# Making the key product's input mixtures between the tiles of rates, in the second half of a two-layer trunk

## The chip, the cores and the metric

The kernel runs on one core of a Trainium2 chip (trn2). The metric is the device time of one execution in microseconds. The kernel before the change takes 2615.0 us, the median of 3 runs (2613.59 to 2615.41). The profiled execution is a run of its own: it took 2623.95 us, and its span from the first to the last instruction is 2621.8 us, at a mean granted TensorE clock of 0.965.

## The reference: what is computed

The input is 1024 frames of 1024 channels. Layer 0 is an RWKV-7 time mixer, layer 1 a diagonal state-space layer. Each is followed by a dense MLP with a squared ReLU, and each of the four sub-layers ends in a layer norm. The change lies in the projections of the time mixer:

```python
xx = jnp.pad(x, ((0, 0), (1, 0), (0, 0)))[:, :-1] - x      # the frame before, less this one
xr = x + xx * mu[0]
xw = x + xx * mu[1]
xk = x + xx * mu[2]
xv = x + xx * mu[3]
xa = x + xx * mu[4]
xg = x + xx * mu[5]
r = xr @ wr
w_pre = (w0 + jnp.tanh(xw @ w1) @ w2).astype(f32)
k = xk @ wk
v = xv @ wv
a = jax.nn.sigmoid(a0 + (xa @ a1) @ a2)
g = jax.nn.sigmoid(xg @ g1) @ g2
```

The decay `w` and the rate `a` come from two small products in a row ("rates" below), the gate `g` likewise ("gates"), and `r`, `k`, `v` each from one 1024 x 1024 product of a mixture of each frame with the frame before it. A recurrence over the frames (`lax.scan`) then uses r, w, k, v and a, head by head.

## The kernel before, in words

**Layout.** Channels lie on the 128 partitions, so that 1024 channels are 8 tiles, and frames lie along the free axis. The frames are worked off in two halves (H = 0 and 1) of 512. A float32 product is made as three fp32r matmuls: each operand is split into a high and a low part (`split`, L152: ScalarE casts the high part in L153, VectorE or GpSimd subtracts it in L154), and `mm3` (L201) multiplies high by high, high by low and low by high. Nearly all matmuls are recorded at L199.

**Projections.** `rwkv_proj(H)` (L253) makes one half's r, w, k, v, a and g and stores them in DRAM. In the second half it works in this order:

1. It splits the 8 tiles of x into operands (L313), and makes three first small products of x (`scaled` L319, `shifted` L334, `gate_c` L360, `gate_a` L379), whose results are the operands `hx` (for the rates), `gx` and `h2` (for the gates).
2. `rates(n)` (L393) for n = 0 to 7: six matmuls of half depth into two PSUM tiles, a Tanh (L404) and a scaling (L349) on ScalarE for each of the two, and two stores (L389).
3. `gate(n)` (L408) for n = 0 to 7: four matmuls, a copy on ScalarE (L421), a store.
4. The key product: `mixes(2)` (L287) makes the 8 mixtures, one per tile of channels, and `squares` (L432) multiplies them with two column blocks of the weight at a time (48 matmuls for a pair, evacuated by L442). Then the same for r with `mixes(0)`, and last for v with `mixes(3)`.

**One mixture** (`mixes`, L287 to L301): ScalarE multiplies the tile by 1 - mu (L290). For odd tiles VectorE adds mu times the shifted tile (L292, one instruction). For even tiles ScalarE makes mu times the shifted tile in a second buffer (L295) and GpSimd adds the two (L296). Then `operand(m)` splits the sum, so that ScalarE casts it to `oAh` (L153) and VectorE subtracts for `oAl` (L154). A mixture issues no DMA.

**Buffers.** `oAh` and `oAl` have 8 slots each. The operands of x fill all of them until the first small products are done. Then `hx`, `gx` and `h2` take three of `oAh`, which leaves five, and `hx` comes free after the last rate, `gx` and `h2` after the last gate. `m` has 2 slots. The tag `ev`, from which the second buffer of an even mixture and every evacuated rate or gate comes, has 4.

**Order.** The order in which the instructions stand in each engine's queue is not the written one. A planner of the framework (the kernel is built with `schedule_with_timeline_sim=True`) lays it out ahead of time: it takes ready instructions by priority, hands out slots, and goes by durations of its own. Priorities rise in the order of writing, and `rank(base)` (L89) starts a stretch at a given number, where a lower number goes first. `core()` (L801) ranks the recurrence of each eighth m (`elem` L514, `amat` L591, `invert` L627, `chain` L689, `gnorm` L745) at m x 10000 and a few thousand, and both halves' projections at 100000, the second half's being written at m = 3. So the projections are what fills the engines beside the recurrence. `wo(0)` (L968, rank 99000) and the first layer norm (L861, rank -1) follow for the first half, written at m = 5, and then the MLP.

Of the kernel before, what the change touches and what calls it, by code (L numbers as in the profile page):

```python
# [73 lines left out]
def trunk(ctx, tc, A):  # L74
# [13 lines left out]
    @contextmanager  # L88
    def rank(base):  # L89

        keep = tc.cur_priority
        tc.cur_priority = base
        yield
        tc.cur_priority = keep
# [19 lines left out]
    def vec(n, k):  # L114
        i = PV.index(n)
        return pv[:, i, k : k + 1]
# [35 lines left out]
    def split(src, hi, lo, e=None):  # L152
        S.copy(hi, src)  # L153
        (e or V).tensor_sub(lo, src, hi.bitcast(F32))  # L154
# [12 lines left out]
    def wload(src, kt, n, key=None):  # L167

        step = 512 // n
        out = []  # L170
        for k0 in range(0, kt, step):
            kept = low.get((key, k0)) if key else None
            raw = wp.tile([128, step, n], F32, tag="wraw", name="wraw", bufs=2)
            SP.dma_start(raw, src[:, k0 : k0 + step])
            hi = wp.tile([128, step, n], F32R, tag="whi", name="whi")
            lo = wp.tile([128, step, n], F32R, tag="wlo", name="wlo")
            nw[0] += 1
            if kept is not None:
                SP.dma_start(lo.bitcast(F32).rearrange("p k n -> p (k n)"), kept)
                S.copy(hi, raw)  # L180
            else:
                split(raw, hi, lo, G if nw[0] % WLG[0] in WLG[1] and WLG[2] <= nw[0] < WLG[3] else V)
                if key:
                    low[key, k0] = dr.tile([128, 512], F32, name=f"low{len(low)}")
                    SP.dma_start(low[key, k0], lo.bitcast(F32).rearrange("p k n -> p (k n)"))
            out += [(hi[:, k], lo[:, k]) for k in range(step)]
        return out
# [10 lines left out]
    def mmb(p, w, x, **kw):  # L198
        bulk.append((PE.matmul(p, w, x, **kw).ins, x.shape[-1]))  # L199

    def mm3(p, whi, wlo, xh, xl, first, last):  # L201
        mmb(p, whi, xh, start=first, stop=False)
        mmb(p, whi, xl, start=False, stop=False)
        mmb(p, wlo, xh, start=False, stop=last)
# [28 lines left out]
    def operand(src, H=0, e=None):  # L233
        h, l = optile(H, "h"), optile(H, "l")
        split(src, h, l, e)
        return h, l

    def psd():
        return pd.tile([128, HT], F32, tag="d", name="d")
# [13 lines left out]
    def rwkv_proj(H):  # L253
# [25 lines left out]
        def spare0():  # L279
            t = spare("vsa", 2, 2) + spare("vsa", 2, 2)  # L280
            for _ in range(4):
                t += spare("kbt", 1, KTB)
            t += [stash[:, k, l] for k in (1, 2, 3) for l in range(2)]
            t += spare("o", 1, OB) + spare("o", 1, OB)
            return [(t[2 * k], t[2 * k + 1]) for k in range(KT)]

        def mixes(j, dst=None):  # L287
            for k in range(KT):
                m = tp.tile([128, HT], F32, tag="m", name="m")
                S.mul(m, xs[k][:, 1:], mum[:, j, k : k + 1])  # L290
                if k % 4 in VM[H]:
                    V.scalar_tensor_tensor(m, xs[k][:, 0:HT], vec(f"mu{j}", k), m, op0=ALU.mult, op1=ALU.add)  # L292
                else:
                    m2 = tp.tile([128, HT], F32, tag="ev", name="m2", bufs=EVB)
                    S.mul(m2, xs[k][:, 0:HT], vec(f"mu{j}", k))  # L295
                    G.tensor_add(m, m, m2)  # L296
                if dst:
                    split(m, *dst[k])
                    yield dst[k]
                else:  # L300
                    yield operand(m)  # L301
# [13 lines left out]
        if H == 0:  # L315
            with rank(MIXR):
                xm = list(mixes(2))
# [30 lines left out]
        def half_sigmoid(t):  # L348
            S.activation(t, t, AF.Identity, bias=half, scale=0.5)  # L349
# [38 lines left out]
        def store_out(out, n, e):  # L388
            (ST if out in STO else SP).dma_start(scr[out][n * 128 : (n + 1) * 128, t0 : t0 + HT], e)  # L389
# [3 lines left out]
        def rates(n):  # L393

            if n % 4 == 0:
                w2[0] = wload(A["wa2"][:, n // 4], 4, 128, f"wa2{n}")
            pp = [psd(), psd()]
            for wi, xi in ((0, 0), (0, 1), (1, 0)):
                for j in range(2):
                    js = slice(64 * j, 64 * j + 64)  # L400
                    mmb(pp[j], w2[0][n % 4][wi][js], hx[xi][js], start=wi == 0 and xi == 0, stop=wi == 1)
            for j, out in ((0, "sg"), (1, "a")):
                e = tp.tile([128, HT], F32, tag="ev", name="ev", bufs=EVB)
                S.activation(e, pp[j], AF.Tanh, bias=pvh[:, j, n : n + 1], scale=0.5)  # L404
                half_sigmoid(e)
                store_out(out, n, e)

        def gate(n):  # L408
            if n % 4 == 0:
                wg[0] = wload(A["g2a"][:, n // 4], 4, 128, f"g2a{n}")  # L410
                rawb = wp.tile([128, 512], F32, tag="wraw", name="w2raw", bufs=2)
                SP.dma_start(rawb, A["g2b"][:, n * 128 : n * 128 + 512])
                wg[1] = wp.tile([128, 512], F32R, tag="whi", name="w2st")
                S.copy(wg[1], rawb)
                V.tensor_sub(wg[1][64:128], rawb[64:128], wg[1][64:128].bitcast(F32))
            q = n % 4
            p = psd()
            mm3(p, wg[0][q][0], wg[0][q][1], gx[0], gx[1], True, False)
            mmb(p, wg[1][:, q * 128 : (q + 1) * 128], h2, start=False, stop=True)
            e = tp.tile([128, HT], F32, tag="ev", name="ev", bufs=EVB)  # L420
            S.copy(e, p)  # L421
            store_out("g", n, e)

        def square(wn, out, xm, n):
            p = psd()
            w = [x for k0 in (0, 4) for x in wload(A[wn][n][:, k0 : k0 + 4], 4, 128, f"{wn}{n}-{k0}")]
            dense(p, w, xm)
            e = tp.tile([128, HT], F32, tag="ev", name="ev", bufs=EVB)
            S.copy(e, p)  # L429
            store_out(out, n, e)  # L430

        def squares(wn, out, xm, n):  # L432

            pp = [psd(), psd()]
            for k0 in (0, 4):
                ws = [wload(A[wn][n + j][:, k0 : k0 + 4], 4, 128, f"{wn}{n + j}-{k0}") for j in range(2)]
                for k in range(4):
                    for j in range(2):
                        mm3(pp[j], *ws[j][k], *xm[k0 + k], k0 + k == 0, k0 + k == KT - 1)
            for j in range(2):  # L440
                e = tp.tile([128, HT], F32, tag="ev", name="ev", bufs=EVB)
                S.copy(e, pp[j])  # L442
                store_out(out, n + j, e)

        if H == 0:

            km = xm
            with rank(MIX0R):
                rm = list(mixes(0, spare0()))
            for n in range(4):  # L450
                rates(n)
                square("wk", "k", km, n)
            for n in range(4):
                square("wr", "r", rm, n)
            yield
            for n in range(4, KT):
                rates(n)
                square("wk", "k", km, n)
            for n in range(4, KT):
                square("wr", "r", rm, n)  # L460
            if not GV:
                for n in range(KT):
                    gate(n)
        else:
            for n in range(KT):
                rates(n)
            for n in range(KT):
                gate(n)
            for j, wn, out in ((2, "wk", "k"), (0, "wr", "r")):
                xm = list(mixes(j))  # L470
                for n in range(0, KT, 2):
                    if n in (0, 2, 4, 6):
                        squares(wn, out, xm, n)
                    else:
                        square(wn, out, xm, n)
                        square(wn, out, xm, n + 1)
# [324 lines left out]
    def core():  # L801

        pg = rwkv_proj(0)
        next(pg)
        bulk.clear()
# [8 lines left out]
        for m in range(8):  # L814
            if m == PB:
                with rank(100000):
                    run(rwkv_proj(1))
# [700 lines left out]
    for c in range(2):  # L1518
        for b in range(JB - TB, JB):
            db(b, False, slice(256 * c, 256 * c + 256))  # L1520
        if c == 0:
            with rank(LN8R):
                early = last_norm(hB, 3, 0)
# [74 lines left out]
```

## Time and profile before

| | before |
|---|---|
| median of 3 runs | 2615.0 us |
| profiled execution: its time, its span | 2623.95 us, 2621.8 us |
| granted TensorE clock, mean | 0.965 |
| TensorE matmul, busy | 2483.8 us, 95% |
| VectorE, busy | 1812.8 us, 69% |
| ScalarE, busy | 1215.2 us, 46% |
| GpSimd, busy | 492.9 us, 19% |

PE is the matmul engine, DVE VectorE, ACT ScalarE, POOL GpSimd, SP SyncE, whose queue (SPq) issues the loads and stores. A row of the waits names the instruction that waited, the one that released it, the microseconds, how often and the longest. A row of stretches gives for each engine the busy microseconds and the instructions, then PEclk (the granted TensorE clock as a share of full speed), the share of time in which the DMA engines were busy, and GB/s. A row of groups gives line, engine, operation, tiles written and read, shapes and count, then busy us and mean ns of one, then the idle time ahead of them and what ended it. A row of the timeline starts with the start and the length in us. Times within the run count from the first instruction.

In that count, second-half rates are evacuated by ScalarE from 320.0 to 362.8 us, the second half's gates are evacuated until 376.6, the first pair of key columns is evacuated at 412.9 and 413.9, the last pair of r is stored at 541.2, and the last of v at 653.4.

### The profile page before, as it was taken

Reading aid. Unit: us, or ns where it says so; the run is one execution under the profiler, and the core shown is the slowest. Engines: PE = TensorE matmul, PEld = TensorE weight load, DVE = VectorE, ACT = ScalarE, POOL = GpSimd, SP = SyncE. Lnnn points to the kernel's source line nnn. Section 1 sums busy time; section 2 is a strip of 40 time slices with the busy share of each in tenths; the row PEclk is TensorE's granted clock in tenths of the full one; section 3 lists DMA queues with packets and bytes.
Section 4 is the critical chain, followed back from the end, with each engine's and each line's share of the span. In section 5 each row is a group of like instructions: output and inputs, shape, how many; then the busy total and the mean of one; then the engine's idle time right before and its main releaser. Section 6 shows DMA issues by size and latency. Waiting matters only on the chain.

```text
span 2621.8 us, 43716 instructions
## 1 busy us (share of the span) xinstructions
PE 2483.8 (95%) x16624; PEld 2013.9 (77%) x16624; DVE 1812.8 (69%) x3299; ACT 1215.2 (46%) x2171; POOL 492.9 (19%) x404
## 2 busy tenths in 40 slices
PE   7899979999989999999999999999999999999997
PEld 5778757788767787777787888887777888888876
DVE  7367767576987777899886555677687555555576
ACT  7554575555454443445543333433464333423344
POOL 3121442433431202001000000101212111111011
PEclk9998979988979999999999999999999999999998
DMA  4764555555322333446655333253222111111123
GB/s 145 257 215 153 169 186 171 181 172 172 105 64 84 97 91 105 162 121 157 182 195 181 96 96 97 93 178 136 93 85 83 54 49 53 53 49 57 49 93 116
DMA packets 207569, 320.72 MB, mean 122 GB/s; under 512 B 20352, under 2 KB 81920, under 8 KB 207360
## 3 DMA queue, kind: packets, MB, share of 16 engines
q1 hardware_dynamic: 206208, 315.84, 38.2%
q8 instruction: 131, 2.15, 0.3%
q10 hardware_dynamic: 1152, 2.10, 0.2%
q14 instruction: 78, 0.64, 0.1%
HBM read 253.89 MB, written 63.96 MB: 121 GB/s over the span
## 4 chain that ended last, share of the span: by engine, by line
PE 57%; DVE 9%; DMA 3%; issue 2%; ACT 2%; POOL 0%; SPq 0%; DVEq 0%; ACTq 0%; POOLq 0%
PE d L199 43%; PE d L1046 9%; DVE wlo L154 2%; DMA wraw<-in_mw_dram 1%; DMA s_y<-yg 1%; DVE hA L1009 1%; ACT hA L905 0%; PE pu L1318 0%; PE pbu L1330 0%; ACT whi L153 0%; PE py L1382 0%; PE py L1390 0%; DMA yl<-s_y 0%; DVE hB L904 0%; PE pk L1279 0%
## 5 line engine op out<-in xcount | busy, mean ns | idle before, releaser
L153 ACT CAST whi<-wraw 128x512 fp32r<-128x512 f32 x524 | 324.5, 620 | 678.0 <-PE d L199 429.3
L154 DVE TENSOR_TENSOR wlo<-wraw,whi 128x512 fp32r<-128x512 f32 x524 | 392.8, 750 | 251.9 <-ACT whi L153 244.6
L199 PE MATMUL d<-qbuf,whi 128*128 128x512 f32 (+1 forms) x1344 | 407.2, 386 | 13.1 <-DVE hA L1009 7.1
L199 PE MATMUL d<-oAh,whi 128*128 128x512 f32 (+1 forms) x768 | 310.9, 412 | 14.2 <-ACT ev L429 7.8
L199 PE MATMUL d<-oAh,wlo 128*128 128x512 f32 (+1 forms) x768 | 309.4, 408 | 7.2 <-DVE wlo L154 4.3
L199 PE MATMUL d<-oAl,whi 128*128 128x512 f32 (+1 forms) x768 | 309.0, 407 | 7.0 <-DVE oAl L154 7.0
L199 PEld LDWEIGHTS d<-qbuf,whi 128*128 128x128 f32 x1344 | 244.0, 188 | 69.1 <-DVE hA L1009 11.2
L199 PE MATMUL d<-qbuf,wlo 128*128 128x512 f32 (+1 forms) x672 | 255.7, 383 | 1.6 <-DVE wlo L154 1.4
L199 PE MATMUL d<-oBh,wlo 128*128 128x512 f32 x512 | 203.4, 398 | 3.5 <-DVE wlo L154 3.4
L199 PE MATMUL d<-oBh,whi 128*128 128x512 f32 x512 | 201.5, 394 | 2.3 <-ACT whi L153 2.2
L199 PE MATMUL d<-oBl,whi 128*128 128x512 f32 x512 | 200.2, 391 | 0.0
L199 PEld LDWEIGHTS d<-oAh,whi 128*128 128x128 f32 (+1 forms) x768 | 148.1, 195 | 50.2 <-ACT ev L429 10.0
L199 PEld LDWEIGHTS d<-oAh,wlo 128*128 128x128 f32 (+1 forms) x768 | 148.0, 194 | 41.2 <-DVE wlo L154 5.8
L199 PEld LDWEIGHTS d<-oAl,whi 128*128 128x128 f32 (+1 forms) x768 | 148.1, 194 | 39.8 <-DVE oAl L154 9.9
L199 PE MATMUL d<-qh,wlo 128*128 128x512 f32 x384 | 151.3, 394 | 0.0
L199 PE MATMUL d<-ql,whi 128*128 128x512 f32 x384 | 150.6, 392 | 0.0
L199 PE MATMUL d<-qh,whi 128*128 128x512 f32 x384 | 149.2, 389 | 0.0
L199 PEld LDWEIGHTS d<-qbuf,wlo 128*128 128x128 f32 x672 | 126.3, 188 | 28.3 <-DVE wlo L154 3.0
L1009 DVE TENSOR_TENSOR hB<-hB,d 128x512 f32<-128x512 f32 (+1 forms) x168 | 104.8, 632 | 30.1 <-PE d L199 28.2
L199 PEld LDWEIGHTS d<-oBh,wlo 128*128 128x128 f32 x512 | 96.2, 188 | 28.4 <-DVE wlo L154 6.1
L1009 DVE TENSOR_TENSOR hA<-hA,d 128x512 f32<-128x512 f32 x144 | 97.3, 680 | 28.1 <-PE d L199 27.0
L199 PEld LDWEIGHTS d<-oBh,whi 128*128 128x128 f32 x512 | 96.2, 188 | 23.7 <-ACT whi L153 2.8
(478 smaller groups left out, 5137.4 us busy)
## 6 DMA issues: line engine op xcount, KB each, us to landing
wraw<-in_mw_dram SPq DMA_DIRECT2D x376, 256.0 KB, 2.7
wraw<-in_glu_dram SPq DMA_DIRECT2D x64, 256.0 KB, 2.7
low<-wlo SPq DMA_DIRECT2D x52, 256.0 KB, 2.8
wlo<-low SPq DMA_DIRECT2D x52, 256.0 KB, 3.7
raw<-in_mw_dram SPq DMA_DIRECT2D x48, 256.0 KB, 2.6
wraw<-in_wk_dram SPq DMA_DIRECT2D x32, 256.0 KB, 3.4
wraw<-in_wr_dram SPq DMA_DIRECT2D x32, 256.0 KB, 3.9
wraw<-in_wv_dram SPq DMA_DIRECT2D x32, 256.0 KB, 4.5
```

What stands on the lines that cost most here:

```text
L153: S.copy(hi, src)
L154: (e or V).tensor_sub(lo, src, hi.bitcast(F32))
L199: bulk.append((PE.matmul(p, w, x, **kw).ins, x.shape[-1]))
L1009: V.tensor_add(z, z, p)
L1046: PE.matmul(p, w[:, k], x, start=not add and k + j == 0, stop=k == 3 and j == 2, skip_group_check=True)
```

## The change: what it does

Only the second half's branch of `rwkv_proj` is edited. The generator of the key product's mixtures is opened ahead of the rates. One mixture is taken from it after each of the rates 0 to 4, a sixth after rate 7, and the last two after the gates. The key product then uses this list and makes no mixtures of its own. The work of each mixture, the number of instructions, the products and the r and v parts are the same as before. What is moved is the place in the order of writing, and so the priority.

```diff
         else:
+            early = mixes(2)
+            km = []
             for n in range(KT):
                 rates(n)
+                if n < 5:
+                    km.append(next(early))
+            km.append(next(early))
             for n in range(KT):
                 gate(n)
+            km += list(early)
             for j, wn, out in ((2, "wk", "k"), (0, "wr", "r")):
-                xm = list(mixes(j))
+                xm = km if j == 2 else list(mixes(j))
                 for n in range(0, KT, 2):
                     if n in (0, 2, 4, 6):
                         squares(wn, out, xm, n)
```

## The prediction

> **What bounds the kernel now.** I read the page first, for the whole, then the busy time by stretches around the second half's projections, then who waited for whom inside the two stretches that the change touches.
>
> ```profile
> span 2621.8 us, 43716 instructions
> PE 2483.8 (95%) x16624; PEld 2013.9 (77%) x16624; DVE 1812.8 (69%) x3299; ACT 1215.2 (46%) x2171; POOL 492.9 (19%) x404
> ```
>
> PE bounds the run as a whole: 2483.8 of 2621.8 us. The change takes no matmul away, so it can gain only where PE stands idle or runs at a lowered clock. The stretches show where that is.
>
> ```profile
> core 0: us, PE busy (x) PEld busy (x) DVE busy (x) ACT busy (x) POOL busy (x), PEclk, DMA share, GB/s
> 318.00:376.00 58.00, 48.56 (x550) 37.51 (x549) 34.94 (x69) 43.00 (x81) 19.14 (x15) 0.82 0.59 195
> 376.00:414.00 38.00, 28.17 (x170) 21.80 (x170) 36.84 (x69) 23.39 (x42) 24.59 (x18) 0.78 0.42 136
> 414.00:460.00 46.00, 45.28 (x438) 35.41 (x435) 29.79 (x86) 25.31 (x48) 5.81 (x5) 1.00 0.60 197
> 655.00:800.00 145.00, 125.61 (x1156) 101.15 (x1153) 131.09 (x260) 70.67 (x132) 62.31 (x47) 0.86 0.26 83
> 800.00:1050.00 250.00, 249.74 (x1879) 200.48 (x1878) 176.27 (x329) 106.11 (x191) 39.72 (x32) 1.00 0.32 97
> ```
>
> The first row is the stage of the rates and gates, the second the one in which the key product's mixtures are made and its first pair of columns is multiplied. In the second, DVE is full (36.84 of 38 us) and PE is starved: 9.8 us idle, and the granted clock is at 0.78. In the first, DVE has 23.1 us to spare and ACT 15.0. From 414 on PE is full at clock 1.00. So the mixtures are made in the one place where DVE has no room, and PE pays for it. The timeline of ACT and of DVE shows the mixtures' first and last steps and what they hold up.
>
> ```profile
> 376.03 0.59 ACT L421 COPY ev<-d 128x512 f32<-128x512 f32 x1 [0.33 <-PE d L199]
> 381.77 1.13 ACT L153 CAST oAh<-m 128x512 fp32r<-128x512 f32 x2
> 412.86 0.58 ACT L442 COPY ev<-d 128x512 f32<-128x512 f32 x1
> 388.11 0.66 DVE L154 TENSOR_TENSOR oAl<-m,oAh 128x512 fp32r<-128x512 f32 x1
> 406.61 0.68 DVE L154 TENSOR_TENSOR oAl<-m,oAh 128x512 fp32r<-128x512 f32 x1
> ```
>
> The last gate is copied out at 376.0. The first two mixtures are cast from 381.8, and the second is complete at 388.8 us. The eighth is complete at 407.3, and the first column of keys is copied out at 412.9. The recurrence has the lower rank numbers, so on DVE its steps go ahead of the mixtures.
>
> **The change, part by part.** The work moved is priced by the groups of the second stretch, which holds eight of each step.
>
> ```profile
> L290 ACT ACTIVATE m<-xs,mum 128x512 f32<-128x512 f32 x8 | 5.7, 722 | 4.5 <-DVE oAl L154 4.4
> L153 ACT CAST oAh<-m 128x512 fp32r<-128x512 f32 x8 | 4.8, 615 | 5.8 <-DVE m L292 4.5 <-POOL m L296 1.3
> L295 ACT ACTIVATE m<-xs,pv 128x512 f32<-128x512 f32 x4 | 2.7, 714 | 0.0
> L154 DVE TENSOR_TENSOR oAl<-m,oAh 128x512 fp32r<-128x512 f32 x8 | 5.7, 709 | 0.0
> L292 DVE SCALAR_TENSOR_TENSOR m<-xs,pv,m 128x512 f32<-128x512 f32 x4 | 5.1, 1276 | 0.1
> L296 POOL TENSOR_TENSOR m<-m,m 128x512 f32<-128x512 f32 x4 | 6.2, 1554 | 2.3 <-DVE oAl L154 1.4 <-ACT m L290 0.9
> ```
>
> Six of eight mixtures are 6/8 x (5.7 + 4.8 + 2.7) = 9.9 us of ACT, 6/8 x (5.7 + 5.1) = 8.1 us of DVE and 3/4 x 6.2 = 4.7 us of POOL. (Two of the eight L290 already belong to r, and two of k were made earlier still, so the count comes out alike.) No DMA moves.
>
> *What the second stretch gives back.* I work it out in two ways. First, from PE: of its 38 us, 9.8 are idle, and the 28.2 busy ones ran at 0.78, so that 6.2 of them are clock that was not granted. That leaves 38 - 9.8 - 6.2 = 22.0 us of matmuls at full clock, a saving of at most 16.0. Second, from the mixtures: only two of eight are left after the gates. In the run before, the first two were complete at 388.8, and the eighth at 407.3, so the operands are whole 18.5 us earlier if two late ones take as long as the first two did. The third row of PE's waits, L622 for kbt, and the first, L584 for kf, are the recurrence's own:
>
> ```profile
> PE pb L584 <- POOL kf L579: 3.3, 1, 3.3
> PE d L199 <- DVE oAl L154: 3.2, 2, 2.1
> PE pT L622 <- ACT kbt L624: 2.6, 2, 2.0
> ```
>
> Directly, PE waited for a mixture only 3.2 us. The 3.3 and the 2.6 go only if the planner puts key matmuls into them, which it can do once six mixtures are ready. The ends are therefore 3.2 and 18.5 us. I take 17, near the upper end, because both workings meet there and because the row after it, 414 to 460, shows that PE fed by finished mixtures runs at 45.28 of 46 us. What comes late next is the last two mixtures; the matmuls of the first six (36 of a pair's 48) hide them.
>
> The clock is the part that could be doubted. The rows show 0.78 where PE idles and 1.00 where it doesn't. The Trainium skill (TensorE: Matmul & The Clock Gate, Part 1) makes this a rule: the clock is halved after an idle window and restored by sustained work. If it were instead to stay at 0.78 in the shorter stretch, the page's rule failing, the 22.0 us would take 28.2, and this term would be 9.8 in place of 16.0.
>
> *What the first stretch pays.* ACT has 43.0 + 9.9 = 52.9 us to do in 58, DVE 43.0, POOL 23.8. Each fits, so the lower bound of the cost is nothing; ACT's idle time is the cover. Its largest pieces are waits that the mixtures fill only if they stand ahead of the waiting instruction in ACT's queue:
>
> ```profile
> ACT kf L567 <- DMA lda<-s_a: 4.8, 1, 4.8
> ACT osq L761 <- DVE o L759: 2.2, 1, 2.2
> ACT E L561 <- DVE ldsg L558: 2.0, 1, 2.0
> ACT ev L404 <- DMA s_a<-ev: 1.1, 1, 1.1
> ```
>
> If none of it is filled, the rates and gates end 9.9 us later. And mixtures bring waits of their own: in the second stretch ACT idled 4.5 us ahead of L290 and 5.8 ahead of L153, 10.3 for eight, so 7.7 for six. That puts the upper bound at 17.6. I take 5.0, half of the ACT work: the stretch is nearest to its own row, with 15.0 us idle, and DVE, which ended 8.9 of the 10.3 us of those waits, has time here. Queued behind a waiting mixture on ACT are the next rates' evacuations (for which PE waits, as they free PSUM) and the recurrence's copies; behind a late rate on SP stand its two stores, and behind those the recurrence's loads, one of which already cost DVE's and ACT's time above. An even mixture also holds one of four `ev` slots until POOL has added it. ACT waited for such a slot once, 1.1 us (`ev` L404 on the store of a), so I put nothing on that.
>
> *What is left at the end.* Behind 414 the projections follow each other on PE, and neither `wo(0)` nor the layer norm behind it is reached before them. They move up by 17 - 5 = 12 us. From 655 to 800, with `wo(0)` and the layer norm, DVE is at 131.09 of 145 us and PE waits for it, so an earlier start meets a DVE with 10% to spare. If DVE decided there alone, all 12 would be lost; but 8.1 us of DVE's work left the full stretch, and the recurrence's steps behind it move up too. I take 2 us as lost. Behind 800 PE is full at clock 1.00 (249.74 of 250), and what arrives earlier stays earlier.
>
> The sum: 17 - 5 - 2 = 10 us. Against the profiled execution's 2623.95 us (its span is 2621.8, with 2.15 around it) that is 2613.95. That execution is 8.95 above the median of 2615.0 us, so the forecast in timed runs is **2605.0 us**.
>
> **The rivals.**
>
> *The rates stretch by what the keys save.* All of ACT's 9.9 us and the 7.7 of waits land in the first stretch, 17.6 against 17: 2615.6 us. For it: ACT's idle time there comes from loads and DVE, and is not free room unless the order happens to fit. Against it: DVE is at 60% there, and those waits ended mostly with DVE. To this I count that the gain is swallowed by the full DVE from 655 to 800 (12 lost of 12), and that the planner, which doesn't keep the written order, leaves the mixtures at the gates' end for want of an `ev` slot: 2615.0 each.
>
> *Slower: even mixtures caught behind POOL.* POOL works in order too, and the recurrence's instructions there wait long:
>
> ```profile
> POOL rn L550 <- DVE rn L549: 15.8, 2, 9.8
> POOL vr L765 <- DVE vr L764: 4.7, 1, 4.7
> ```
>
> Should each of the three even mixtures stand behind such a wait (7.9 us on average), both `m` slots are taken, the next L290 stalls, and with it all of ACT. That costs 9.9 + 3 x 7.9 = 33.6 in the first stretch against 17 saved, so 16.6 more: 2631.6 us. It decides once the stalls pass 7.1 us, and shows as slower by over 0.2% from 12.3. Against it: a mixture without its inputs ready is not what the planner takes first, and POOL is busy only 19.14 of 58 us. The Trainium skill (TensorE: Matmul & The Clock Gate, Architectural detail) states the rule that speaks against this change: the queues of ACT, DVE and POOL are strict first-in-first-out. By that rule the trace agrees: on ACT the rates' next evacuation (L404) comes only after the 4.8 us wait of L567 for a load, in two rows of the timeline:
>
> ```profile
> 343.56 0.60 ACT L567 ACTIVATE kf<-lda,kam,pv 128x256 f32<-128x256 f32 x1 [4.81 <-DMA lda<-s_a]
> 346.36 1.26 ACT L404 ACTIVATE ev<-d,pvh 128x512 f32<-128x512 f32 x2
> ```
>
> *More than forecast.* No stretching at all, and nothing lost behind: 2598.0 us. It is the favourable end of the forecast, not a case of its own.
>
> **How the numbers follow.** About 0.2% (5.2 us) is what a measurement of this kernel can tell from no change. The forecast has a chance of 0.62. Its own range is 2598 to 2609: 17 kept whole at one end, and at the other the upper half of the stretching (9 us and 2 lost). No change to speak of has 0.22, of which 0.14 are for rates that stretch and 0.08 for the other two. Slower has 0.16. The range, 2594 to 2620, reaches below the favourable end by 4 us for a recurrence that gains half of the 8.1 us of DVE by itself, and above no change by 5 for a mild case of POOL's stalls; some 0.07 lie under it and 0.12 above.
>
> **What would show it.** In the profile of the changed kernel, L153 `oAh<-m` should stand six times ahead of the last gate's L421, with ACT near 53 us busy up to there. The gates should end by 376 to 384 us, and the first L442 should come near 400 in place of 412.9. The stretch between the two should have a PEclk near 0.95 and no L199 waiting for `oAl` over 1 us. The last store of v should come some 10 to 12 us before 653.4, where it starts here:
>
> ```profile
> L498 SPq DMA_DIRECT2D s_v<-evv x16: 370/419/1062, 201.2 to 653.4; - x16
> ```
>
> The forecast is wrong if the gates end after 390, if the first L442 stays behind 408, or if the last store of v is early and the time unchanged: then the loss lies between 655 and 800.

## The result, and the profile after

The change makes the kernel slower. In timed runs side by side it takes 2639.28 us (median of 6, 2631.5 to 2640.63) against 2618.18 us for the kernel before (median of 6, 2613.59 to 2624.13): a ratio of 1.0068, 95% interval 1.0053 to 1.0084. The forecast was 2605.0 us, 10 us faster, with 2594 to 2620 as its range. The profiled execution of the changed kernel took 2639.24 us with a span of 2637.5 us, 15.7 us more than before's 2621.8.

Lines of `kernel.py` behind L470 stand 6 higher in the changed kernel: before's L712, L716, L722, L723, L726, L881 are its L718, L722, L728, L729, L732, L887. Experiments that are written like the kernel before keep before's numbers.

The head of the page after:

```profile
span 2637.5 us, 43700 instructions
PE 2491.0 (94%) x16624; PEld 2016.2 (76%) x16624; DVE 1821.6 (69%) x3299; ACT 1213.4 (46%) x2171; POOL 491.1 (19%) x404
```

PE is busy for 7.2 us more with the same 16624 matmuls, and idle for 8.5 us more (2637.5 - 2491.0 = 146.5 against 2621.8 - 2483.8 = 138.0). To see where, both runs are cut at the same milestones: 2 us ahead of the first rate, then the ends of the last gate, the first key column, the last key column, the last column of r, the last column of v and the last scaling of the first layer norm, and the start of the MLP's relu number 20. The stretches of before (in the prediction's rows the first three end at 376, 414 and 460):

```profile
core 0: us, PE busy (x) PEld busy (x) DVE busy (x) ACT busy (x) POOL busy (x), PEclk, DMA share, GB/s
318.00:376.60 58.60, 48.95 (x552) 37.66 (x550) 35.54 (x70) 43.57 (x83) 19.70 (x16) 0.83 0.58 194
376.60:413.40 36.80, 27.18 (x156) 21.05 (x158) 35.67 (x66) 22.22 (x41) 24.03 (x18) 0.77 0.42 136
413.40:459.60 46.20, 45.88 (x448) 36.01 (x446) 29.99 (x86) 25.51 (x50) 5.81 (x5) 1.00 0.60 196
459.60:540.95 81.35, 72.90 (x725) 57.24 (x726) 43.86 (x81) 42.30 (x82) 31.74 (x25) 0.94 0.60 185
540.95:651.30 110.35, 105.59 (x1197) 95.47 (x1194) 83.78 (x179) 61.20 (x117) 38.73 (x32) 0.87 0.55 167
651.30:756.90 105.60, 89.29 (x899) 71.41 (x899) 93.59 (x177) 48.61 (x93) 47.44 (x36) 0.84 0.27 84
756.90:1007.70 250.80, 247.72 (x1871) 199.34 (x1870) 186.00 (x369) 113.27 (x206) 46.96 (x38) 0.99 0.31 93
sum 689.70, PE 637.51 PEld 518.19 DVE 508.43 ACT 356.68 POOL 214.41; mean PE 91.07 PEld 74.03 DVE 72.63 ACT 50.95 POOL 30.63
```

And of the changed kernel:

```profile
315.00:376.30 61.30, 51.08 (x467) 39.72 (x466) 41.27 (x63) 49.84 (x94) 23.66 (x18) 0.72 0.55 187
376.30:389.00 12.70, 12.70 (x84) 10.09 (x83) 9.84 (x29) 8.41 (x17) 5.98 (x6) 1.00 0.55 167
389.00:453.05 64.05, 61.38 (x653) 48.28 (x653) 38.13 (x85) 27.90 (x55) 17.59 (x15) 0.95 0.57 180
453.05:552.30 99.25, 85.78 (x834) 65.79 (x830) 66.25 (x143) 52.50 (x100) 36.22 (x28) 0.90 0.49 156
552.30:658.80 106.50, 96.51 (x1127) 87.17 (x1128) 81.52 (x186) 57.75 (x110) 42.16 (x34) 0.90 0.57 174
658.80:772.50 113.70, 91.56 (x885) 74.60 (x884) 93.19 (x160) 49.08 (x94) 43.13 (x34) 0.84 0.26 83
772.50:1024.90 252.40, 247.60 (x1847) 196.71 (x1847) 185.76 (x364) 111.29 (x202) 45.88 (x36) 0.99 0.29 91
sum 709.90, PE 646.63 PEld 522.35 DVE 515.95 ACT 356.76 POOL 214.62; mean PE 92.38 PEld 74.62 DVE 73.71 ACT 50.97 POOL 30.66
```

The reader is to see four things. The rates and gates stretch by 2.7 us. The stretch that was aimed at is 24.1 us shorter, with PE full at clock 1.00 (12.70 of 12.70). The next two give it all back, and more: 64 for 46, and 99 for 81. The layer norm's stretch is 8.1 longer. Over all seven the changed kernel takes 20.2 us more, 9.1 of them busy (646.63 - 637.51) and 11.1 idle. It begins 3 us earlier, is 17 late at relu 20, and ends 15.7 late. (The start says nothing of the change: before and three of the experiments, p1, p7 and q3, have one order of all else up to the first rate, and reach it between 312.9 and 320.0 us.) Behind relu 20 both take the same: 1614.1 us before, 1612.6 after. All that happens, happens ahead of it.

Most signposts of the prediction are there. The row of the high parts' casts (operation, count, shortest, median and longest ns, first and last start) and four rows of ScalarE's timeline:

```profile
L153 ACT CAST oAh<-m x8: 603/614/620, 324.3 to 380.9; 128x512 fp32r<-128x512 f32 x8
```

```profile
359.31 0.61 ACT L153 CAST oAh<-m 128x512 fp32r<-128x512 f32 x1
...
375.70 0.58 ACT L421 COPY ev<-d 128x512 f32<-128x512 f32 x1
380.41 1.14 ACT L153 CAST oAh<-m 128x512 fp32r<-128x512 f32 x2
...
388.41 0.58 ACT L442 COPY ev<-d 128x512 f32<-128x512 f32 x1
```

Six casts stand ahead of the last gate, the gates end at 376.3, and the first key column comes at 388.4 where 400 was forecast. But the last store of v starts late instead of 10 to 12 us early:

```profile
L504 SPq DMA_DIRECT2D s_v<-evv x16: 370/410/2707, 200.9 to 658.8; - x16
```

So the lead of 24.5 us at the first key column (412.9 against 388.4) was lost before v was done, ahead of the place (655 to 800) to which the prediction had tied its doubt.

### The profile page after: what moved, and what is told of

It reads as the page before. It is cut to its first block, busy times and chain, and to the rows that moved or that the text cites. A ratio compares the mean times of both kernels' runs of the same rounds, so it can differ in the third digit from the quotient of the medians.

```text
span 2637.5 us, 43700 instructions
## 1 busy us (share of the span) xinstructions
PE 2491.0 (94%) x16624; PEld 2016.2 (76%) x16624; DVE 1821.6 (69%) x3299; ACT 1213.4 (46%) x2171; POOL 491.1 (19%) x404
## 4 chain that ended last, share of the span: by engine, by line
PE 66%; DVE 15%; DMA 8%; ACT 5%; issue 4%; POOL 1%; SPq 1%; ACTq 0%; DVEq 0%; POOLq 0%
PE d L199 49%; PE d L1052 9%; DVE wlo L154 3%; DMA wraw<-in_mw_dram 1%; ACT whi L153 1%; DVE oAl L154 1%; DVE xh L660 1%; DVE x L658 1%; PE pA L614 1%; DVE KB L584 1%; DMA ldr<-s_r 1%; PE pR L722 1%; DVE hA L1015 1%; PE py L1388 1%; DVE KB L583 0%
## 5 line engine op out<-in xcount | busy, mean ns | idle before, releaser
L199 PE MATMUL d<-qbuf,whi 128*128 128x512 f32 (+1 forms) x1344 | 408.2, 387 | 13.4 <-DVE hA L1015 6.0
L199 PE MATMUL d<-oAh,whi 128*128 128x512 f32 (+1 forms) x768 | 314.7, 415 | 22.9 <-ACT ev L404 7.3
L199 PE MATMUL d<-oAh,wlo 128*128 128x512 f32 (+1 forms) x768 | 312.5, 412 | 8.9 <-DVE wlo L154 8.4
L199 PE MATMUL d<-oAl,whi 128*128 128x512 f32 (+1 forms) x768 | 311.7, 409 | 5.8 <-DVE oAl L154 5.7
L199 PEld LDWEIGHTS d<-qbuf,whi 128*128 128x128 f32 x1344 | 243.4, 188 | 69.4 <-DVE hA L1015 9.3
L199 PE MATMUL d<-qbuf,wlo 128*128 128x512 f32 (+1 forms) x672 | 256.1, 383 | 1.8 <-DVE wlo L154 1.6
L199 PE MATMUL d<-oBh,wlo 128*128 128x512 f32 x512 | 204.1, 399 | 3.0 <-DVE wlo L154 3.0
L199 PE MATMUL d<-oBh,whi 128*128 128x512 f32 x512 | 203.0, 397 | 0.9 <-ACT whi L153 0.7
L199 PE MATMUL d<-oBl,whi 128*128 128x512 f32 x512 | 201.7, 394 | 0.0
L199 PEld LDWEIGHTS d<-oAh,whi 128*128 128x128 f32 (+1 forms) x768 | 149.2, 196 | 61.7 <-ACT ev L429 9.1
L199 PEld LDWEIGHTS d<-oAh,wlo 128*128 128x128 f32 (+1 forms) x768 | 149.5, 196 | 44.3 <-DVE wlo L154 10.8
L199 PEld LDWEIGHTS d<-oAl,whi 128*128 128x128 f32 (+1 forms) x768 | 149.0, 195 | 38.5 <-DVE oAl L154 8.1
L199 PE MATMUL d<-qh,wlo 128*128 128x512 f32 x384 | 151.5, 395 | 0.0
L199 PE MATMUL d<-ql,whi 128*128 128x512 f32 x384 | 150.7, 392 | 0.0
L199 PE MATMUL d<-qh,whi 128*128 128x512 f32 x384 | 149.4, 389 | 0.0
L199 PEld LDWEIGHTS d<-qbuf,wlo 128*128 128x128 f32 x672 | 126.2, 188 | 28.2 <-DVE wlo L154 3.8
L199 PEld LDWEIGHTS d<-oBh,wlo 128*128 128x128 f32 x512 | 96.6, 189 | 27.7 <-DVE wlo L154 4.7
L199 PEld LDWEIGHTS d<-oBh,whi 128*128 128x128 f32 x512 | 96.9, 189 | 22.8 <-issue 1.3
```

## The experiments: the mixtures' place, or the order of all the rest

The planner lays out every engine's queue anew for the changed program. Two things therefore differ between the kernels: where the 36 instructions of the key product's mixtures stand, and how all others stand to each other. The experiments separate them by pinning: for each engine a list of its instructions is written into the kernel, and each is made to follow the one before it in the list, so that the planner has nothing left to choose. The loop stands at the end of the program (ORDER, the lists, is left out here):

```diff
+    traced = {i.name: i for i in nc.cur_bb.bb.instructions}
+    for text in ORDER:
+        names = np.frombuffer(zlib.decompress(base64.b85decode(text)), dtype="<i4").cumsum()
+        row = [traced[f"I-{n}"] for n in names]
+        for x, y in zip(row, row[1:]):
+            tc.add_manual_dep(y, x.name, mybir.DependencyInfo(
+                mybir.DependencyClass.NoSync, mybir.DependencyReason.DATA), reason="order")
```

The dependency carries no semaphore. Mixtures that aren't in a list stand where the planner puts them by their place in the writing.

**Four corners.** `p1` is written like the changed kernel, with ORDER the whole program of before without the key mixtures. `p3` is the other corner: written like before, ORDER the whole program of the changed kernel without them.

> The six mixtures stand early, as in the changed kernel, and every other instruction keeps the order that it had on its engine in the kernel before. Theory A (the change itself saves what was forecast up to the first key column, and the order that the planner makes of everything behind it loses it again): 5 to 20 us faster than before, first key column by 398 us, last store of v by 645. Theory B (the early mixtures cost the time themselves, because ScalarE's queue holds up the recurrence behind them): 10 to 25 us slower than before, like the changed kernel. Theory C (the recurrence sets the end of the projections, whatever the projections do): within 5 us of before, with the last store of v within 3 us of 653.

> The mixtures stand behind the gates, as in the kernel before, and every other instruction keeps the order that it has in the changed kernel. Theory A: the order alone costs, so at least as slow as the changed kernel, 20 to 40 us over before. Theory B: without early mixtures nothing is lost, within 6 us of before. Theory C: within 6 us of the changed kernel.

Measured: p1 0.9998 [0.9983, 1.0013], p3 1.0063 [1.0042, 1.0084]. Early mixtures in the old order cost nothing and bring nothing (p1 is theory C's case). The new order costs 0.6% with the mixtures as late as in the kernel before: the sign of theory A, though some 17 us and not 20 or more. Its first key column comes at 397.2, 15.6 us sooner than in the kernel before, with the mixtures where they always were: most of the early key column wasn't the mixtures' doing.

`p2` and `p4` put the seam at the first pair of key columns. `p2`: written like the changed kernel, ORDER of before from the first pair on. `p4`: written like before, ORDER of the changed kernel from there.

> The changed kernel, but from the first pair of key columns on every engine keeps the order of the kernel before; up to there the planner's own order stands, as in the changed kernel. Theory A: 5 to 20 us faster than before, first key column at 389 to 395 us. Theory B: 10 to 25 us slower than before. Theory C: within 5 us of before.

> The kernel before, but from the first pair of key columns on every engine keeps the order of the changed kernel. Theory A: 15 to 40 us slower than before. Theory B: within 6 us of before. Theory C: within 6 us of before or of the changed kernel.

Measured: p2 1.0019 [1.0007, 1.0031], p4 1.0061 [1.0037, 1.0085]. p4 is written like before, with late mixtures, and carries the whole loss: the order from the first pair on is enough for it. (p4 isn't before itself up to there. What that order sets behind the pair can't come ahead of it, so the first key column comes at 395.8.) p2 has the early key column (388.5) and the old order behind it, and its last key column ends at 461.3, 1.7 us later than before's: the lead is gone within one product. By then p2 and before have run the same number of the recurrence's matmuls, some 880, of which 416 in p2 and 568 in before stood ahead of the first key column.

What p1 shows of the stretches themselves, in the same cut (rates and gates, first key column, last key column):

```profile
316.50:382.10 65.60, 53.25 (x552) 40.78 (x550) 42.98 (x79) 51.74 (x97) 24.78 (x19) 0.74 0.50 172
382.10:412.00 29.90, 23.14 (x156) 18.89 (x158) 27.74 (x57) 13.11 (x24) 18.93 (x15) 0.83 0.55 170
412.00:459.05 47.05, 45.91 (x448) 35.93 (x444) 29.90 (x86) 25.48 (x49) 5.80 (x5) 1.00 0.62 193
```

Before has 58.6, 36.8 and 46.2 there, 141.6 in all, and p1 has 142.6: 7 us paid in the rates, 7 won in the keys, 1 given back. PE's waits in the second row of p1 say why it was only 7:

```profile
PE pb L590 <- POOL kf L585: 4.8, 1, 4.8
PE pT L628 <- ACT kbt L630: 1.4, 2, 0.7
```

The waits for mixtures (3.2 us before) are gone. The recurrence's own, which were 3.3 and 2.6, are still there as 4.8 and 1.4. They belong to the order.

**Where the order loses.** `p5` keeps the changed kernel's order up to the last key column, `p6` up to the last column of v, and both go on in before's. `q3` is the opposite: written like before, before's order up to the last column of v, the changed kernel's behind it.

> The changed kernel, but from the last key column on (ahead of r's mixtures) every engine keeps the order of the kernel before. Theory A (the loss lies in the order of the recurrence's steps among the mixtures and products of r and v, and in the layer norm's stretch behind them): 0 to 8 us faster than before, last store of v by 650. Theory D (the loss was made ahead of r already, and shows only later): 8 to 20 us slower than before.

> The changed kernel, but behind the last column of v every engine keeps the order of the kernel before, so that only wo, the layer norm and what follows are put back. Theory A: the part of the loss that is made by the end of v stays, 5 to 11 us slower than before, and the 8 us of the layer norm's stretch are gone. Theory E (the layer norm's stretch alone makes the loss, and v's lateness is made up for by the recurrence's lead): within 4 us of before.

> The kernel before, with its late mixtures and its order up to the last column of v; behind that every engine keeps the order of the changed kernel. It is the counterpart of the run that put back only what lies behind v. Theory A (the changed order behind v costs by itself): 6 to 13 us slower than before, with v's last column unmoved and the layer norm 6 to 10 us later. Theory G (that stretch is slow in the changed kernel only because of what it inherits): within 5 us of before.

Measured: p5 1.0073 [1.0050, 1.0096], p6 1.0041 [1.0026, 1.0056], q3 1.0058 [1.0035, 1.0081]. p5's figure is theory D's, but its trace shows another loss: a seam costs by itself, because the new order has the recurrence at another point than the old one expects. PE stood still there for 16.8 us, in one piece:

```profile
PE pU L732 <- ACT vsa L729: 16.8, 1, 16.8
```

What stood ahead was VectorE's: the inversion's serial steps (L658, L660), which start at 457.7. The copy that was at last let through, and the step behind it:

```profile
471.01 0.43 DVE L728 COPY vsa<-pX 64x256 f32<-64x256 f32 x1
471.47 0.27 DVE L660 TENSOR_TENSOR xh<-xh,x 128x99 f32<-128x99 f32 x1
```

PE's next step needs the copy of `pX` into `vsa`, and that copy stands in the queue behind 13 us of steps of some 0.2 to 0.3 us each. So p5 tells of its seam and not of the place of the loss. p6 and q3 tell more: with the changed order only up to v 0.41% is lost, and only behind v 0.58% (15 us, where theory A had 6 to 13). They don't add up to 0.68%, and each has a seam of its own. Counts of PE's matmuls show what the seams do. From the first cut to the end of v the changed kernel runs 3155, before and q3 3069, p6 3074: its recurrence is 86 matmuls further on at v's end. So its own tail, from there to the norm's last scaling, takes 113.7 us for 885 matmuls, and q3's 119.3 for 971 (before: 105.6 for 899).

**One wait in the tail.** In the layer norm's stretch PE's two largest waits are these in the changed kernel, and the largest one before is the one that follows:

```profile
PE pU L732 <- ACT vsa L729: 10.5, 3, 7.9
PE pR L722 <- ACT vsa L718: 6.1, 2, 3.9
```

```profile
PE pR L716 <- ACT vsa L712: 4.0, 1, 4.0
```

The timeline of VectorE, ScalarE and PE around the longest:

```profile
733.54 4.87 DVE L887 TENSOR_TENSOR hA<-hA,pm 128x512 f32<-128x512 f32 x8
...
740.24 0.43 DVE L728 COPY vsa<-pX 64x256 f32<-64x256 f32 x1
```

```profile
742.22 0.37 ACT L729 COPY vsa<-pX 64x256 f32<-64x256 f32 x1
```

```profile
734.10 0.68 PE L727 MATMUL pX<-o,XT 64*64 64x64 f32 x16
742.64 1.12 PE L732 MATMUL pU<-vsa,kbt 128*64 128x64 f32 x16 [7.86 <-ACT vsa L729]
```

`pX` is there at 734.8, and its two copies stand behind the norm's eight subtractions and squares. The Trainium skill (TensorE: Matmul & The Clock Gate, Architectural detail) has ScalarE, VectorE and GpSimd as strict first-in-first-out queues. The trace agrees: both copies had their input for over 5 us before they ran. `r1` moves these two alone, in the changed kernel with its own order pinned (not code, but the two engines' queues by source line):

```diff
 DVE  L887 x2
+DVE  L728
 DVE  L887 x6, L765, L618 x2
-DVE  L728
 ACT  L891
+ACT  L729
 ACT  L891, L894 x3, L767, L649 x4
-ACT  L729
```

> The changed kernel with its own order of instructions on every engine, but for two: VectorE's copy of pX into vsa stands behind the second of the first layer norm's eight subtractions, where it stood behind all eight, and ScalarE's copy of the other half stands behind the norm's first square, where it stood behind five squares and four copies. Theory G (the order behind v loses in that place, where PE stood 7.9 us at pU): that wait falls under 2 us, the last scaling of the norm comes 4 to 8 us sooner against the start of wo than in the changed kernel, and the time is 4 to 8 us under the changed kernel's, 1.0037 to 1.0053 of before. Theory H (the recurrence is late all over, and whoever is late waits in another place): the wait goes, PE waits as long further on, and the time stays at 1.006 to 1.008.

Measured: 1.0054 [1.0038, 1.0071], an interval that covers the changed kernel's 1.0068 and most of theory G's figures, so that the time doesn't decide. The trace does:

```profile
734.40 0.68 PE L732 MATMUL pU<-vsa,kbt 128*64 128x64 f32 x16 [1.01 <-ACT vsa L729]
748.36 1.12 PE L722 MATMUL pR<-vsa,AT 128*64 128x64 f32 x16 [12.05 <-ACT vsa L718]
```

The wait of 7.86 is down to 1.01, and the next step of the recurrence waits for 12.05 instead. The norm's last scaling ends 44.9 us behind the start of the last addition of `wo` (771.1 - 726.2), as in the changed kernel (772.5 - 727.6), and the span is 2637.4 against 2637.5 us. So it goes as theory H has it: this one wait is not the cause. The stretch kept its length, and PE's idle time in it only changed its place. That the recurrence is late all over is not shown by it, though. The next steps of the recurrence still stand behind the norm's work: in r1 the product `pU` is done at 735.1, and VectorE's use of it (L735) runs at 744.5. Whether the stretch would shrink with all of them moved, no run shows.

**Is any new order bad?** `n5` is the kernel before with each gate written right behind its rate, mixtures late. `n3` takes the six mixtures in a block between the last rate and the first gate. In both the planner lays out everything anew. The edits, n5's against the kernel before and n3's against the changed one:

```diff
             for n in range(KT):
                 rates(n)
-            for n in range(KT):
                 gate(n)
```

```diff
             for n in range(KT):
                 rates(n)
-                if n < 5:
-                    km.append(next(early))
-            km.append(next(early))
+            km += [next(early) for _ in range(6)]
             for n in range(KT):
```

> The kernel before, with each gate written right behind its rate and the mixtures left behind the gates; the planner lays everything out anew, and 254 in place of 151 of the recurrence's matmuls come to stand between the first and the last column of r (276 in the changed kernel). Theory A (a new order is enough to lose): 5 to 20 us slower than before, with r's eight columns taking over 58 us in place of 51. Theory B (early mixtures are needed for the loss): within 5 us of before.

> Six mixtures are written in one block between the last rate and the first gate, none between the rates. 252 of the recurrence's matmuls stand among r's columns. Theory A: first key column 10 to 25 us early, and the time nevertheless 3 to 20 us slower than before. Theory B (the mixtures between the rates are what costs): within 5 us of before or faster.

Measured: n5 0.9999 [0.9989, 1.0009], n3 1.0002 [0.9988, 1.0016]. That is theory B's time for both: a new order as such need not lose anything, so that the 0.6% belongs to the order of this kernel. n3 has its first key column 16.9 us early and ends where before ends. n5 was 14 us ahead at the norm and level at the end. A lead in the projections doesn't reach the end in either of them. Nor does a long r stretch settle the time: it takes 93.5 us in n5 and 95.1 in n3 (81.4 before, 99.3 in the changed kernel), 13.1 and 10.6 of them idle, and both make up for it elsewhere.

`p10` asks what takes the lead, with early mixtures and before's order on all engines but PE, which is free:

> Early mixtures; ACT, DVE, POOL and SP keep the order of the kernel before for everything else, and PE's order alone is the planner's. Theory F (with PE's order held the mixtures are worth some 7 us there, because PE then waits for the recurrence's kf and kbt; with PE free the first key column comes early, but the serial inversion on DVE still sets when the recurrence lets PE go on, so that the lead is gone by the last key column): first key column by 402 us, last one within 4 us of 459.6, time within 6 us of before. Forecast's step (what arrives earlier stays earlier): last key column 8 us early or more, 5 to 12 us faster.

Measured: 1.0019 [1.0005, 1.0033]. The first key column ends at 404.9, 8.5 us early (402 was expected), and the last one at 457.3, 2.3 early. The profiled run reaches the first rate 5.1 us sooner than before's, so from there the first column is only 3.4 us early, and the last is 2.8 late. With PE's order alone laid out anew, some of the key matmuls go ahead of the recurrence's (528 in place of 568 of these stand ahead of the first key column), and nothing of the lead is left when both are done.

**A smaller dose.** `n2` takes only two mixtures early, behind rates 0 and 1 (all six others after the gates). `p7` is the same with all else pinned to before's order, and `s1` has the mixtures late and all else in n2's order. n2's edit against the changed kernel:

```diff
-                if n < 5:
+                if n < 2:
                     km.append(next(early))
-            km.append(next(early))
             for n in range(KT):
                 gate(n)
```

> Two mixtures early, the rest behind the gates, and the planner lays everything out anew; 225 of the recurrence's matmuls come to stand among r's columns (151 before, 276 in the changed kernel). Theory A (the new order of the rest decides, whatever is moved): r's eight columns take 55 us or more in place of 51, and the time is 0 to 12 us slower than before. If the number of early mixtures decided: a third of the changed kernel's loss, 5 to 6 us slower.

> Only the first two mixtures are made early, between the first rates, and every other instruction keeps the order of the kernel before. Theory F: the rates and gates lengthen by 1 to 3 us in place of 5.5, PE's direct waits for mixtures (3.2 us) shrink by half or more; 0 to 4 us faster than before. Theory C (nothing there can move the time): within 2 us of before.

> Two mixtures behind the first two rates, everything else laid out anew, once more: the earlier run gave 0.9988, with an interval that took in 1. If two early mixtures gain something that can be measured, this run lies at 0.998 to 0.9995 again; if that was chance, at 1.000 to 1.001.

> The kernel before, all eight mixtures late, with every other instruction on every engine in the order that the planner laid out for two early mixtures (the kernel that ran at 0.9978). Theory I (its gain, too, is the order's, and the place of two mixtures is worth nothing): 0.997 to 0.9995. Theory J (the gain needs both, two mixtures early and an order that fits them): 1.000 to 1.003.

Measured: n2 0.9988 [0.9972, 1.0004] and again, with more runs, 0.9978 [0.9964, 0.9992]; p7 1.0015 [1.0002, 1.0027], a miss; s1 1.0015 [1.0003, 1.0026]. Neither of the two times expected of n2 came true, and r's columns take 52.6 us in the first and 55.1 in the second (51 before). Two early mixtures in the old order are a little slower, n2's order with late mixtures as well, and the two together are a little faster. So here, other than with six, place and order gain only together (theory J), unless the pins themselves cost the 0.15%: no run pins n2's own order with its mixtures early, and p1's interval would leave room for 0.13%. n2 beats both kernels, by 0.22% against before in the second measurement. The sum of its profile there, over the same stretch, 2 us ahead of the first rate to relu 20:

```profile
sum 683.15, PE 633.59 PEld 513.42 DVE 507.09 ACT 355.33 POOL 214.86; mean PE 633.59 PEld 513.42 DVE 507.09 ACT 355.33 POOL 214.86
```

683.2 against 689.7 us, of which 3.9 fewer are busy and 2.6 fewer idle.

## Why the prediction was wrong, step by step

**The term of 17 for the keys was mis-sized.** With the order held it measured 7 in p1 (36.8 to 29.9). Both workings made the same mistake. The one from PE took all 9.8 us of idle time and 6.2 of clock as the mixtures' doing, the one from the mixtures took all 18.5 us between the second and the eighth as time for which PE had to wait. The row that bore on it was quoted: PE waited for a mixture for only 3.2 us. The two other waits were the recurrence's, and I let the planner fill them. It did so in the changed kernel, where the stretch is 24.1 us shorter, but not for nothing.

**The price of the rates, 5, was about right** for the order held (7 in p1, with ScalarE at 51.74 us in 65.6). In the changed kernel the stretch is only 2.7 us longer, and holds less work: 467 of PE's matmuls where before has 552. One thing in it I had put at nothing, the `ev` slots. ScalarE's waits there:

```profile
ACT ev L421 <- DMA s_sg<-ev: 2.4, 1, 2.4
ACT m L295 <- DMA s_sg<-ev: 2.3, 1, 2.3
```

An even mixture and a gate each waited for a rate's store, 4.7 us in all, on an engine that was busy for 49.84 of 61.30 us.

**The step that failed is the sentence "They move up by 17 - 5 = 12 us", and with it "what arrives earlier stays earlier".** It took the projections as a row of matmuls that moves up as one. They share PE with the recurrence. (Nor was PE full "from 414 on": that reading rests on the row up to 460, and in before's r stretch PE is busy for 72.90 of 81.35 us.) The rows of L199 alone, which holds the projections' matmuls, before and after (PE's busy time and count first):

```profile
318.00:413.40 95.40, 42.30 (x140) 26.64 (x140) 0.80 0.52 172
413.40:459.60 46.20, 33.11 (x132) 24.09 (x132) 1.00 0.60 196
459.60:540.95 81.35, 52.17 (x192) 36.21 (x192) 0.94 0.60 185
```

```profile
315.00:389.00 74.00, 37.01 (x133) 24.77 (x134) 0.77 0.55 183
389.00:453.05 64.05, 39.08 (x141) 25.79 (x139) 0.95 0.57 180
453.05:552.30 99.25, 56.46 (x192) 37.59 (x192) 0.90 0.49 156
```

Taken from all of PE's matmuls, the rest is the recurrence's. Up to the first key column that is 708 - 140 = 568 before and 549 - 133 = 416 after (467 and 84 in the rows above, where two that cross the cut count twice): 152 were put off. From there to the last key column it is 316 before and 512 after: 196 more. The 24 us won became 18 lost in the next stretch. In the r stretch another 109 came in (642 against 533), and there the new order did worse than repay: of its 17.9 us more, 8.6 are the recurrence's busy time, 4.3 are the same 192 matmuls of the product (56.46 against 52.17), and 5.0 are idle (99.25 - 85.78 against 81.35 - 72.90). The granted clock, 0.90 against 0.94, makes some 2.3 of the 4.3, by an estimate from these rows (52.17 x 0.94 / 0.90 = 54.5). Put off and repaid would have been the same time. The idle time and the longer matmuls are the loss in that stretch, and in this kernel nothing behind it makes up for them.

**The "2 lost" from 655 to 800 was the wrong kind of loss.** I had asked what an early arrival loses to a full DVE there. What came was a late arrival and a stretch 8.1 us longer, 5.8 of it idle, by the order (q3, with before's projections ahead of it, loses there too).

**The slower rival named a time near the result and a mechanism that isn't there.** Even mixtures were not caught behind POOL: the gates end at 376.3, 2.7 us of stretch and not 33.6, and ScalarE waits in that stretch for nothing on POOL. That the changed kernel, 21 us slower than before, comes near the rival's 16.6 is chance. What was missing is a rival in which the planner's new order, over 600 us of shared queues, is worse than the old one. The prediction named the planner as the one who fills waits, who might leave the mixtures where they were and who takes first what is ready, and never priced that it lays out all the rest again.

**Open.** p1, p3 and p4 show that the order is the cause. Why the planner, which goes by its own durations, chose one that is worse on the chip, no run shows. No run pins a kernel to the whole of its own order, so the price of a pin by itself is bounded only by p1 (0.9998 of before) and by r1 (its span within 0.1 us of the changed kernel's). That the 86 matmuls are all of why p6 and q3 don't add up is not shown. Nor is it shown what in n2 makes place and order fit.

## What to carry to other kernels

Where a planner orders the queues, an edit's effect is that of the instructions moved plus that of all others laid out anew: pin the old order to learn the first, and put a term for the second into the range (here -0.2% to +0.7% for four small edits of one place, where the moved instructions by themselves were worth 0 to 0.15%). An early milestone is no gain while other work shares the bound engine: count that work up to the milestone, and sum PE's busy and idle time over a stretch that ends where both kernels run alike again. Before giving an idle stretch to an edit, look at which waits in it are for the thing that is moved; here 3.2 of 9.8 us were.

## What the runs showed of the hardware

VectorE's copy of half a state into `vsa` takes 0.29 us (the median of 32 in the changed kernel), but one in the layer norm took 2.39. Rows of the changed kernel, GpSimd's and VectorE's:

```profile
746.18 1.26 POOL L895 TENSOR_TENSOR sq<-sq,sq 128x512 f32<-128x512 f32 x1
747.40 1.26 POOL L787 TENSOR_TENSOR vt<-vt,lg 128x512 f32<-128x512 f32 x1
```

```profile
746.42 2.39 DVE L719 COPY vsa<-st 64x256 f32<-64x256 f32 x1
...
749.30 0.29 DVE L719 COPY vsa<-st 64x256 f32<-64x256 f32 x1
```

The long copy starts inside the first of two GpSimd instructions that follow each other and ends, at 748.81, with the second (748.66). The Trainium skill (SBUF — State Buffer, SBUF: two separate sides) says that GpSimd and some of VectorE's instructions take turns on a shared pair of ports, which one instruction holds from start to end while the other engine is fully blocked. The rows agree, and show that the loser may stand through two of the other's instructions. r1 has it again, 2.51 us from 744.90 on, beside the same two of GpSimd (744.78 to 747.25). No run takes these two away, so the cause is argued from the times. PE's recurrence waited behind this copy, for 3.9 us.
